# Layer 1's u, k, v and first two q tiles as seven-product quads behind four plain gate tiles, and fewer projection tiles left as filler for the attention and s5 stages

## The chip, the cores and the metric

One core of a Trainium2 chip runs the whole kernel. The metric is device time in microseconds of one launch. The core has a matrix engine (TensorE, PE in the profile; its weight loads are shown apart as PEld), three engines for element work (VectorE or DVE, ScalarE or ACT, GpSimd or POOL), a queue engine SyncE (SP), and DMA. Every engine works through its own instructions in order and waits for the others by semaphores.

## The reference

Two layers over 1024 tokens of width 1024, then a last RMSNorm. All is float32.

```python
hn = rmsnorm(h, norm1_g[layer]); proj = hn @ w_in[layer]      # 1024 x 3328
u, q, k, v = ...                                              # 512, 512, 128, 128 columns of proj
gate_a, gate_b = sigmoid(...), sigmoid(...)                   # 1024 columns each
y_a = s5_branch(u, ...)      # 32 groups of 16 channels, 64 complex states, a scan over the tokens in both
                             # directions, gelu to z, then z * sigmoid(z @ w_glu)
y_b = windowed_gqa(q, k, v, sink, bias, mask)                 # 8 query heads, 2 key heads, window 128
merged = gate_a * (y_a @ w_branch_a) + gate_b * (y_b @ w_branch_b)
h = h + merged @ w_out
hn2 = rmsnorm(h, norm2_g[layer])
h = h + (silu(hn2 @ ffn_w_gate) * (hn2 @ ffn_w_up)) @ ffn_w_down
```

## The kernel before

**Tiles and matmuls.** Activations lie with channels on the 128 partitions and tokens along the free side, in tiles of 128 channels by 512 tokens; the two halves of the tokens are h = 0 and 1. A float32 product is made of three matmuls on operands split into a high and a low part: high by high, low by high, high by low (L176 to L178 in `chain`, L187 to L189 in `piece`). One output tile of a projection, 128 columns of `w_in` by 512 tokens, is 8 k-tiles by 3 = 24 matmuls of 128x512. It is called an item here, `pj` in the profile; two items (both halves) share one weight block, a `Granule`.

**Weights.** A granule is 128x1024 of float32 (512 KB). SP loads it (L125, tile `raw`), ACT makes the high part (L164, `whi`), DVE the low part (L165, `wlo`). `emit` walks the list of items in order and keeps the split a few granules ahead (`ahead`) and the load further ahead (`fetch_to`). Plain float32 tiles live in 86 shared slots of 128x512.

**Quads.** In the FFN, a pair of weight blocks and both token halves are multiplied as a 2x2 block product with seven block products in place of eight. Each block product is 4 k-tiles by 3 = 12 matmuls, so a quad is 84 matmuls where four items are 96. It needs sums of weight blocks (`quad_part`, L139 to L153: tiles `sm`, `s3`, `s4`, `whs`, `wls`) and sums of activations (tiles `y`, then split into `tt`). Before the change only the FFN does this.

**Layer 1's first half, in the order of its list of items.** First the norm (`rs` on DVE at L89, psn on PE at L328 and L305), with the last products of layer 0's FFN (`dn`) laid between its steps. Then the projections k, v, q0, q1 and u0 as plain items. Then `attention_items`: 19 steps, each with score, softmax, transpose (`pt`) and value (`pv`) work, and `per * (i + 1)` filler items handed out in all by step i. Then `s5_items`.

**The s5 stage.** There are 16 states q and 8 outputs i, each output from two states. A state is eight small matmuls on PE (L943, `s5x`; 16 records in the trace), then on DVE nine instructions (L951 to L967) ending in `s5s`, then four copies on ACT (L971, `s5sg`). An output is twelve matmuls on PE (L985 to L988, `s5y`; 24 records); ACT squares and copies it (L990, L991), and its gelu goes DVE L1001 (`s5w`), ACT L1002, DVE L1009 (`s5g`). The result is stored to HBM (L1014, `zd`, four DMAs), and for the last two outputs SP issues those stores. One iteration of the loop holds two states and one output; the output belongs to states made two iterations earlier. Filler items stand between them, 2 for each iteration in layer 1.

**Behind the s5 stage.** `glu_items` loads z back (L1099, SP, `z<-zd`, eight DMAs, two for each of z0 to z3), ACT and DVE split it (`zp0h` to `zp3h` at L113, `zp0l` to `zp3l` at L114), and PE forms 8 glu tiles (96 matmuls), then the branch products `br`, whose operand `ybh` ACT casts (L860), then w_out.

**What sets the order.** The list of items is written by hand, and a scheduler lowers it to one instruction stream for each engine. Which item is filler where is set by the numbers `per` and by the order of the lists in `build`.

Of the kernel before, what the change touches and what calls it, by code (L numbers as in the profile page):

```python
# [8 lines left out]
F32 = mybir.dt.float32  # L9
# [4 lines left out]
ADD, SUB, MUL = ALU.add, ALU.subtract, ALU.mult  # L14
# [7 lines left out]
HC = 512  # L22
# [9 lines left out]
M_U, M_Q, M_K, M_V, M_GA, M_GB = 0, 4, 8, 9, 10, 18  # L32
# [16 lines left out]
R_BUFS = 4  # L49
# [47 lines left out]
class Trunk:  # L97
# [142 lines left out]
    def ahead(self, n):  # L240
        n = min(n, len(self.order))
        while self.split_ < n:

            g = self.order[self.split_]
            self.fetch_to(min(self.split_ + (R_BUFS if isinstance(g, QuadPart) else R_BUFS - 1), len(self.order)))
            self.parts(self.order[self.split_])
            self.split_ += 1

# [433 lines left out]
    apart = None  # L682

    def proj(self, l, m, done, xs=None):

        g = self.w_in(l, m)
        apart = self.apart
        st = {}

        def half(h):  # L690
            def run(part=None):
                if part != 1:
                    st[h] = self.PS(f"pj{m}")
                self.chain(st[h], g, 0, (xs or self.hn)[h], part)
# [173 lines left out]
    def attention_items(self, l, keys, q23, fill, per, tail):  # L868


        stage = {}
        fill = (list(fill[:2]) if l else []) + q23 + list(fill[2 if l else 0:])

        def scores(u):
            stage[u] = self.att_scores(l, u // 8, u % 8)
# [12 lines left out]
        for i in range(19):  # L888
# [232 lines left out]
        return early, split, out  # L1121


    def w_out_items(self, l):
        nc, V = self.nc, self.nc.vector
        self.h2 = {}
# [46 lines left out]
    def ffn_items(self, l, fill, head):  # L1173
# [6 lines left out]
        early = quads < 4  # L1180
# [56 lines left out]
        T = [[None] * 4 for _ in range(4)]  # L1237

        def sums(j):

            at = ((j, 0), (j, 1), (j + 4, 0), (j + 4, 1))
            if early:
                y11, y12, y21, y22 = (ys.pop(a) for a in at)
            else:
                y11, y12, y21, y22 = (self.A("y") for _ in at)
                for y, (m, h) in zip((y11, y12, y21, y22), at):
                    hi, lo = self.hn2[h][m]
                    V.tensor_tensor(y, hi.bitcast(F32), lo.bitcast(F32), ADD)
            V.tensor_tensor(y11, y12, y11, SUB)
            V.tensor_tensor(y12, y22, y12, SUB)  # L1250
            V.tensor_tensor(y22, y22, y11, SUB)
            V.tensor_tensor(y21, y21, y22, SUB)
            for k, y in enumerate((y11, y22, y12, y21)):
                T[k][j] = (y, None)

        def sum_pairs(j, k):
            T[k][j] = self.split(T[k][j][0], f"tt{k}")

        def quad_items(f):

            q = Quad(self.t["w_gate"][l, f].rearrange("p k c -> p (k c)"), self.t["w_up"][l, f].rearrange("p k c -> p (k c)"))
            b = {}

            def product(bank, g, off, xs, start):
                def run():
                    if start:
                        b[bank] = self.PS(f"q{bank}")
                    self.piece(b[bank], g, off, xs(), start)
                return (run, g)

            B = lambda h, a: lambda: self.hn2[h][a:a + 4]
            p = [product("x", q.a, 0, B(0, 0), True), product("y", q.b, HC, lambda: T[1], True),
                 product("v", q.b, 0, lambda: T[0], True), product("x", q.a, HC, B(0, 4), False),
                 product("y", q.c, 0, lambda: T[2], False), product("w", q.d, 0, lambda: T[3], True),
                 product("v", q.e, 0, B(1, 4), False)]

            def first():
                b["p1"] = self.A("qp")
# [101 lines left out]
    def build(self):  # L1380
# [31 lines left out]
        for l in range(DEPTH):  # L1412
# [23 lines left out]
            n0, n1 = (self.norm_parts(h, "ra", 2 * l, lambda m, h=h, src=src: src(m, h), lambda: self.hn) for h in range(2))  # L1436
            v1, v2 = self.halves(vc[0])
            loads, states = self.s5_head(l)
            tail_items = {12: pairs[:1] if l == 0 else []}
# [201 lines left out]
```

## Time and profile before

| | us |
|---|---|
| median of 3 runs | 2642.86 |
| lowest and highest run | 2641.52, 2645.24 |
| profiled execution, own time | 2646.65 |
| profiled execution, span of its trace | 2644.8 |
| PE busy | 2593.0 (98%) |
| DVE busy | 1660.2 (63%) |
| ACT busy | 1065.1 (40%) |

The span is the time from the first to the last instruction of the trace; the execution's own time is 1.85 us longer. Matmuls overlap, and their ends are modelled, so the busy time of PE is not the sum of their durations.

### The profile page before, as it was taken

How to read it: one execution, taken by the hardware profiler on the slowest of the kernel's cores; microseconds unless marked ns; L12 is line 12 of the kernel's file. 1: busy time of each engine (PE TensorE's matmuls, PEld its weight loads, DVE VectorE, ACT ScalarE, POOL GpSimd, SP SyncE). 2: the span in 40 equal slices, each digit the busy share in tenths (PEclk: the TensorE clock that was granted, in tenths of full speed). 3: DMA queues.
4: the chain of work that ended last, by engine and by line, in shares of the span. 5: the costliest groups of instructions: out<-in, count | busy, mean ns of one | idle time of the engine just before them, and what ended most of it. 6: DMA issues, size and time to landing. Idle time of an engine off the chain costs nothing.

```text
span 2644.8 us, 35127 instructions
## 1 busy us (share of the span) xinstructions
PE 2593.0 (98%) x12878; PEld 2109.6 (80%) x12878; DVE 1660.2 (63%) x3333; ACT 1065.1 (40%) x2053; POOL 359.8 (14%) x524
## 2 busy tenths in 40 slices
PE   8999999999999999999999999999999999999997
PEld 6787677887788888888877778888878888888886
DVE  8986877575986745544673465756376644654556
ACT  5336744422443433333344543453235433333332
POOL 0141001000142220121010001200002221122010
PEclk9999999999999999999999999999999999999998
DMA  3453435354274652564342245434315652455243
GB/s 139 131 186 123 136 117 183 118 189 143 60 191 118 124 107 60 115 127 91 103 151 76 72 140 171 149 128 159 128 64 114 133 124 64 90 121 114 59 110 134
DMA packets 157439, 321.36 MB, mean 122 GB/s; under 512 B 20769, under 2 KB 55841, under 8 KB 157265
## 3 DMA queue, kind: packets, MB, share of 16 engines
q1 hardware_dynamic: 106192, 201.68, 23.2%
q0 software_dynamic: 51072, 117.43, 20.4%
q8 instruction: 101, 1.65, 0.3%
q14 instruction: 74, 0.60, 0.1%
HBM read 196.37 MB, written 122.63 MB: 121 GB/s over the span
## 4 chain that ended last, share of the span: by engine, by line
PE 91%; DVE 5%; ACT 2%; DMA 1%; issue 1%; SPq 0%; DVEq 0%; ACTq 0%
PE pj L176 7%; PE pj L177 6%; PE pj L178 6%; PE dn L176 6%; PE dn L177 6%; PE dn L178 6%; PE qy L189 2%; PE qx L189 2%; PE qv L189 2%; PE qy L187 2%; PE qv L187 2%; PE qx L188 2%; PE qy L188 2%; PE qv L188 2%; PE qx L187 2%; PE br L176 2%
## 5 line engine op out<-in xcount | busy, mean ns | idle before, releaser
L165 DVE TENSOR_TENSOR wlo<-raw,whi 128x1024 fp32r<-128x1024 f32 (+3 forms) x210 | 186.5, 888 | 265.1 <-ACT whi L164 254.4
L164 ACT CAST whi<-raw 128x1024 fp32r<-128x1024 f32 (+3 forms) x210 | 163.6, 780 | 364.5 <-PE pj L177 116.5
L176 PE MATMUL pj<-rah,whi 128*128 128x512 f32 x768 | 307.4, 401 | 1.4 <-ACT rah L113 1.0
L177 PE MATMUL pj<-ral,whi 128*128 128x512 f32 x768 | 301.1, 392 | 1.3 <-DVE ral L114 1.3
L178 PE MATMUL pj<-rah,wlo 128*128 128x512 f32 x768 | 300.9, 392 | 0.0
L1220 POOL DMA_DIRECT2D hs<-dx x208 | 179.4, 872 | 854.6 <-ACT dx L1219 755.4
L176 PEld LDWEIGHTS pj<-rah,whi 128*128 128x128 f32 x768 | 145.2, 189 | 37.1 <-issue 4.8
L177 PEld LDWEIGHTS pj<-ral,whi 128*128 128x128 f32 x768 | 145.3, 189 | 31.5 <-DVE ral L114 3.2
L178 PEld LDWEIGHTS pj<-rah,wlo 128*128 128x128 f32 x768 | 145.0, 189 | 31.1
L1219 ACT COPY dx<-dn 128x512 f32<-128x512 f32 x208 | 120.9, 583 | 76.1 <-PE dn L178 75.4
L187 PE MATMUL qx<-rfh,whi 128*128 128x512 f32 x280 | 108.9, 389 | 0.0
L188 PE MATMUL qx<-rfl,whi 128*128 128x512 f32 x280 | 108.9, 389 | 0.0
L189 PE MATMUL qx<-rfh,wlo 128*128 128x512 f32 x280 | 108.9, 389 | 0.0
L799 DVE CUSTOM_DVE_ANT_0 x<-s,bias,nsink 128x384 f32<-128x384 f32 (+1 forms) x128 | 67.5, 580 | 64.0 <-PE s L793 63.7
L971 ACT COPY s5sg<-s5s 64x256 f32<-64x256 f32 x128 | 51.7, 404 | 128.9 <-DVE s5s L966 127.5
L176 PE MATMUL wo<-mgh,whi 128*128 128x512 f32 x256 | 100.0, 391 | 0.0
L178 PE MATMUL wo<-mgh,wlo 128*128 128x512 f32 x256 | 99.6, 389 | 0.0
L177 PE MATMUL wo<-mgl,whi 128*128 128x512 f32 x256 | 99.6, 389 | 0.0
L113 ACT CAST ffah<-ts 128x512 fp32r<-128x512 f32 x35 | 21.7, 621 | 190.3 <-DVE ts L1298 190.3
L176 PE MATMUL dn<-ffbh,whi 128*128 128x512 f32 x232 | 91.3, 394 | 0.0
L177 PE MATMUL dn<-ffbl,whi 128*128 128x512 f32 x232 | 90.6, 391 | 0.0
L177 PE MATMUL dn<-ffal,whi 128*128 128x512 f32 x232 | 90.4, 390 | 0.0
(431 smaller groups left out, 6711.2 us busy)
## 6 DMA issues: line engine op xcount, KB each, us to landing
hs<-dx POOLq DMA_DIRECT2D x208, 256.0 KB, 6.1
raw<-in_w_in SPq DMA_DIRECT2D x52, 512.0 KB
raw<-in_w_gate SPq DMA_DIRECT2D x44, 512.0 KB
raw<-in_w_up SPq DMA_DIRECT2D x44, 512.0 KB
raw<-in_w_down SPq DMA_DIRECT2D x96, 192.0 KB
g<-th POOLq DMA_DIRECT2D x64, 256.0 KB, 2.8
thr<-g SPq DMA_DIRECT2D x64, 256.0 KB
hs<-h POOLq DMA_DIRECT2D x48, 256.0 KB, 2.3
```

The lines of the kernel that those rows point to most:

```text
L164: nc.scalar.copy(g.hi[:, :n], g.raw[:, :n])
L165: nc.vector.tensor_tensor(g.lo[:, :n], g.raw[:, :n], g.hi[:, :n].bitcast(F32), SUB)
L176: mm(ps, lhsT=wh, rhs=xh, start=k == 0, stop=False)
L177: mm(ps, lhsT=wh, rhs=xl, start=False, stop=False)
L178: mm(ps, lhsT=wl, rhs=xh, start=False, stop=k == n - 1)
L187: mm(ps, lhsT=wh, rhs=xh, start=start and k == 0, stop=False)
L188: mm(ps, lhsT=wh, rhs=xl, start=False, stop=False)
L189: mm(ps, lhsT=wl, rhs=xh, start=False, stop=k == len(xs) - 1)
L799: V.tensor_tensor_reduce(out=x[:, :n], in0=ps[:, :n], in1=self.bias[hd][:, bo:bo + n], op0=ADD, op1=ALU.min, scale=-1.0, scalar=self.nsink ...
L971: nc.scalar.copy(SG[64 * r:64 * r + 64, g * 256:(g + 1) * 256].rearrange("p (d n) -> p d n", d=2), Sv[64 * g:64 * g + 64, :, r])
L1219: nc.scalar.copy(t, ps)
L1220: nc.gpsimd.dma_start(self.hs[m, h], t, accum_op=ADD)
```

## The change

**1. `ahead`.** For a plain granule the load is ordered up to two blocks ahead of the split and no longer three. Quad parts keep four.

**2. Layer 1's front.** `linear_quads` turns pairs of output tiles into quads: u0 with u1, u2 with u3, k with v, q0 with q1. It calls the existing tile functions with `grab` set, so that only their `done` functions (what is done with a finished tile) are taken. `sums` and `sum_pairs`, moved out of the FFN, make the activation sums for them, once for all four quads: 16 sums of `y` on DVE and 16 splits `tt`. In front of the quads stand four gate tiles gb0 to gb3, and no longer k and v, while the norm is made.

**3. Filler.** Before, the filler handed to the attention and s5 stages was q2, q3 (4 items), u1 to u3 (6 items) and all sixteen gate tiles (32 items): 42 items, 1 for each attention step and then 2 for each s5 iteration, 2 kept for glu. Now u is done earlier and so are four gate tiles: 28 items remain, 0.9 for each attention step (20 of them), then 1 for each s5 iteration (8), none for glu.

```diff
-            self.fetch_to(min(self.split_ + (R_BUFS if isinstance(g, QuadPart) else R_BUFS - 1), len(self.order)))
+            self.fetch_to(min(self.split_ + (R_BUFS if isinstance(g, QuadPart) else R_BUFS - 2), len(self.order)))
...
+        if self.grab is not None:
+            self.grab.append((m, done))
+            return []
...
-        fill = (list(fill[:2]) if l else []) + q23 + list(fill[2 if l else 0:])
+        fill = q23 + list(fill)
...
-            if i in (5, 7):
+            if i in (5, 7) and keys[-1]:
...
+    def linear_quads(self, l, made, T):
+
+        nc, V = self.nc, self.nc.vector
+        self.grab = tiles = []
+        for f in made:
+            f()
+        self.grab = None
+        out, nxt = [], []
+        for (m1, done1), (m2, done2) in zip(tiles[::2], tiles[1::2]):
+            p, b = self.quad_products(self.t["w_in"][l, m1], self.t["w_in"][l, m2], lambda: self.hn, T)
...
+        for k, (p, e) in enumerate(nxt):
+            if k == 0:
+                out.append(p[0])
+            out += [p[1], e[0], p[2], e[1], p[3], p[4], e[2], p[5], e[3]]
+            if k + 1 < len(nxt):
+                out.append(nxt[k + 1][0][0])
+            out += [e[4], p[6], e[5]]
+        return out
...
-                k1, k2 = self.halves(kc[0])
+                s = [(lambda j=j, T=T, ys=ys: self.sums(T, ys, self.hn, j),) for j in range(4)]
+                sp = [[(lambda j=j, k=k, T=T: self.sum_pairs(T, j, k),) for j in range(4)] for k in range(4)]
...
+                us = self.linear_quads(l, [lambda i=i: self.tile_u(l, i) for i in range(4)], T)
+                kvq = self.linear_quads(l, [lambda: self.tile_kv(l, M_K, kn), lambda: self.tile_kv(l, M_V, vn),
+                                            lambda: self.tile_q(l, 0), lambda: self.tile_q(l, 1)], T)
+                a, c = (self.halves(x) for x in (gb[0], gb[2]))
...
-                         [k1, n1[0], k2, v1, n1[1], n1[2], v2, n1[3], n1[4], n1[5], qc[0], ke[0], ve[0], qe[0], kc[1], ke[1],
-                          vc[1], ve[1]] + keys[:2] + [qc[1], qe[1], vals, bias0] + q1 + us[:2])
-                left = self.attention_items(l, keys, q23, us[2:] + gb + ga, 1, tail_items)
+                         [a[0], n1[0], a[1], c[0], n1[1], n1[2], c[1], n1[3], n1[4], n1[5], gb[4], *s[:2], gb[1], *s[2:], gb[3], *sp[1], gb[5],
+                          *sp[0], gb[6], *sp[2], gb[7], *sp[3]] + us + kvq[:15] + keys + kvq[15:17] + [vals] + kvq[17:] + [bias0])
+                left = self.attention_items(l, [None] * 4, q23, gb[8:] + ga, 0.9, tail_items)
...
-                left = self.s5_items(l, left, 2)
+                left = self.s5_items(l, left, 1)
```

(The lists `gb` and `ga` hold two items for each tile, one for each half; `gb[:8]` are the four tiles.) On PE the s5 stage of layer 1 now runs, from state 6 on: s5x(6), item, s5x(7), s5y(2), s5x(8), s5x(9), item, s5y(3), s5x(10), item, s5x(11), s5y(4), s5x(12), s5x(13), item, s5y(5), s5x(14), item, s5x(15), s5y(6), item, s5y(7), item, and then glu. On DVE, between the first instruction of state 6 and the last of state 15, stand ten states, four gelus and three low parts of weights. Before, PE had an item behind each s5x there, two behind s5y(6), and six between s5y(7) and glu.

The rows that follow are the instruction streams as they are ordered before and after the change; the changed file's line numbers are 3 higher there (L770 is L773, L990 is L993, L1002 is L1005) and 89 higher in the FFN. The first line of the change moves no row on any engine when it is made alone.

ScalarE in layer 1's s5 stage, around the sixth output, before: `s5sg<-s5s` are the copies of a state, `th<-pj` the end of a filler item, `s5g<-s5w` a gelu, `whi<-raw` the high part of a filler's weights.

```order
L1002 ACTIVATE s5g_15417<-s5w_15527 128x512
L770 ACTIVATE th1_15565<-pj12_15540 128x512
L990 ACTIVATE s5g_15588<-s5y_15574 128x512
L991 COPY s5yc_15587<-s5y_15574 128x512
L971 COPY s5sg_15617<-s5s_15611 64x256 x4
L770 ACTIVATE th0_15647<-pj13_15622 128x512
L971 COPY s5sg_15683<-s5s_15677 64x256 x4
L1002 ACTIVATE s5g_15588<-s5w_15688 128x512
L770 ACTIVATE th1_15716<-pj13_15691 128x512
L164 CAST whi_15773<-raw_15490 128x1024
```

The same stretch in the changed kernel:

```order
L993 ACTIVATE s5g_15815<-s5y_15801 128x512
L994 COPY s5yc_15814<-s5y_15801 128x512
L974 COPY s5sg_15844<-s5s_15838 64x256 x4
L974 COPY s5sg_15885<-s5s_15879 64x256 x4
L1005 ACTIVATE s5g_15815<-s5w_15890 128x512
L773 ACTIVATE th0_15928<-pj16_15903 128x512
L993 ACTIVATE s5g_15957<-s5y_15943 128x512
L994 COPY s5yc_15956<-s5y_15943 128x512
L164 CAST whi_16110<-raw_15932 128x1024
L974 COPY s5sg_15986<-s5s_15980 64x256 x4
```

Before, an end of a filler stands between any two groups of state copies; now one filler stands for two states, and two groups of copies follow one another.

ScalarE from the last output of layer 1's s5 stage on, before (`s5g<-s5y` is the last output's square, `zp0h<-z0` the first split of z):

```order
L990 ACTIVATE s5g_15828<-s5y_15814 128x512
L991 COPY s5yc_15827<-s5y_15814 128x512
L770 ACTIVATE th0_15856<-pj15_15831 128x512
L1002 ACTIVATE s5g_15828<-s5w_15866 128x512
L164 CAST whi_15934<-raw_15771 128x1024
L770 ACTIVATE th1_15894<-pj15_15869 128x512
L770 ACTIVATE th0_15928<-pj16_15903 128x512
L164 CAST whi_16034<-raw_15860 128x1024
L770 ACTIVATE th1_15963<-pj16_15938 128x512
L113 CAST zp0h_15979<-z0_15967 128x512
```

The same stretch in the changed kernel:

```order
L773 ACTIVATE th0_16104<-pj17_16079 128x512
L1005 ACTIVATE s5g_16073<-s5w_16076 128x512
L993 ACTIVATE s5g_16133<-s5y_16119 128x512
L994 COPY s5yc_16132<-s5y_16119 128x512
L164 CAST whi_16267<-raw_16108 128x1024
L773 ACTIVATE th1_16161<-pj17_16136 128x512
L1005 ACTIVATE s5g_16133<-s5w_16165 128x512
L113 CAST zp0h_16185<-z0_16173 128x512
L113 CAST zp0h_16189<-z0_16175 128x512
```

Before, one filler's end stands ahead of the last gelu, three stand behind it up to zp0h, and two more behind zp2h; now one stands ahead of it and none behind. ScalarE's line after zp2h then goes straight to the eight casts `ybh` and to zp3h; on VectorE the eight low parts `ybl` stand ahead of `zp3l` in both kernels.

SyncE's DMA issues from the store of the last but one output of layer 1's s5 stage on, before (`zd13` is the last quarter of z in HBM, `raw<-in_...` loads of weights):

```order
L1014 DMA zd13_12482<-s5g_15739 8x16x128 x4
L125 DMA raw_16032<-in_w_br_a 128x1024
L1014 DMA zd13_12482<-s5g_15828 8x16x128 x4
L125 DMA raw_16123<-in_w_br_b 128x1024
L1099 DMA z0_15967<-zd10_12479 128x512
L1099 DMA z0_15969<-zd10_12479 128x512
L1099 DMA z1_15971<-zd11_12480 128x512
L1099 DMA z1_15973<-zd11_12480 128x512
L1099 DMA z2_15975<-zd12_12481 128x512
L1099 DMA z2_15977<-zd12_12481 128x512
L125 DMA raw_16273<-in_w_br_a 128x1024
L1099 DMA z3_16038<-zd13_12482 128x512
L1099 DMA z3_16040<-zd13_12482 128x512
```

The same stretch in the changed kernel:

```order
L1017 DMA zd13_12480<-s5g_16073 8x16x128 x4
L1102 DMA z0_16173<-zd10_12477 128x512
L1102 DMA z0_16175<-zd10_12477 128x512
L1102 DMA z1_16177<-zd11_12478 128x512
L1102 DMA z1_16179<-zd11_12478 128x512
L1017 DMA zd13_12480<-s5g_16133 8x16x128 x4
L1102 DMA z2_16181<-zd12_12479 128x512
L1102 DMA z2_16183<-zd12_12479 128x512
L125 DMA raw_16611<-in_w_br_b 128x1024
L1102 DMA z3_16209<-zd13_12480 128x512
L1102 DMA z3_16211<-zd13_12480 128x512
```

Before, the loads of z0 to z2 follow the last store's four DMAs; now the loads of z0 and z1 stand ahead of those, and those of z2 and z3 behind.

At one more place VectorE's order differs: between the rows of the reciprocal root of layer 1's first half of the tokens (`rs`, L89) and the normed tiles `y` (L342) two sums of weight blocks of the first quad (`sm`, L139 and L140, 128x512) now stand, the first ahead of the last three `rs` rows, the second behind them.

## Rows read from the trace of the kernel before

**Rows 1.** Page of before: span; busy us of each engine (share, instructions); one group of section 5.
```profile
span 2644.8 us, 35127 instructions
...
PE 2593.0 (98%) x12878; PEld 2109.6 (80%) x12878; DVE 1660.2 (63%) x3333; ACT 1065.1 (40%) x2053; POOL 359.8 (14%) x524
...
L971 ACT COPY s5sg<-s5s 64x256 f32<-64x256 f32 x128 | 51.7, 404 | 128.9 <-DVE s5s L966 127.5
```

**Rows 2.** Timeline of PE in layer 1's front: start us, us, engine, line, what.
```profile
1375.62 0.39 PE L176 MATMUL pj<-rah,whi 128*128 128x512 f32 x1
...
1376.98 0.39 PE L176 MATMUL pj<-rah,whi 128*128 128x512 f32 x1
```

**Rows 3.** Windows: us, then busy us of PE, PEld, DVE, ACT, POOL; PEclk; DMA.
```profile
1380.00:1400.00 20.00, 20.00 (x94) 16.65 (x93) 3.68 (x3) 11.74 (x20) 0.00 (x0) 1.00 0.39 119
1639.55:1655.63 16.08, 16.08 (x105) 13.39 (x104) 13.23 (x29) 6.86 (x15) 3.62 (x6) 1.00 0.65 213
454.54:468.08 13.54, 10.79 (x62) 9.35 (x63) 11.88 (x27) 5.88 (x14) 2.37 (x4) 0.75 0.22 65
```

**Rows 4.** Timeline of DVE in layer 1's norm.
```profile
1341.16 0.68 DVE L296 TENSOR_TENSOR sqc<-sqc,sq 128x512 f32<-128x512 f32 x1
```

**Rows 5.** Timeline of PE in layer 1's norm; in brackets the idle time and its releaser.
```profile
1342.64 1.16 PE L328 MATMUL psn<-cst,rs 128*128 128x128 f32 x8 [0.94 <-DVE rs L89]
...
1359.49 0.63 PE L178 MATMUL pj<-rah,wlo 128*128 128x512 f32 x1
...
1365.46 0.63 PE L176 MATMUL pj<-rah,whi 128*128 128x512 f32 x1
```

**Rows 6.** Timeline of PE at a step of layer 0's attention.
```profile
299.77 0.65 PE L839 MATMUL pv<-p,vt 128*64 128x256 f32 x4 [1.54 <-ACT p L826]
```

**Rows 7.** Timeline of PE in one s5 iteration of layer 1.
```profile
1639.55 0.38 PE L985 MATMUL s5y<-s5uk 128*128 128x128 f32 x2
...
1642.32 1.10 PE L943 MATMUL s5x<-s5uk,s5wbt 128*64 128x128 f32 x16
1643.35 0.50 PE L176 MATMUL pj<-rah,whi 128*128 128x512 f32 x1
...
1649.01 1.10 PE L943 MATMUL s5x<-s5uk,s5wbt 128*64 128x128 f32 x16
```

**Rows 8.** Timeline of DVE in one s5 iteration of layer 0.
```profile
454.54 0.69 DVE L1001 SCALAR_TENSOR_TENSOR s5w<-s5g,s5yc 128x512 f32<-128x512 f32 x1
...
457.29 0.68 DVE L951 TENSOR_TENSOR s5a<-s5x,s5tb 128x512 f32<-128x512 f32 x1
...
462.68 0.68 DVE L951 TENSOR_TENSOR s5a<-s5x,s5tb 128x512 f32<-128x512 f32 x1
...
468.08 0.68 DVE L1001 SCALAR_TENSOR_TENSOR s5w<-s5g,s5yc 128x512 f32<-128x512 f32 x1
```

**Rows 9.** Timeline of DVE behind layer 1's s5 stage.
```profile
1732.07 1.23 DVE L165 TENSOR_TENSOR wlo<-raw,whi 128x1024 fp32r<-128x1024 f32 x1 [4.46 <-ACT whi L164]
```

**Rows 10.** Timeline of ACT behind layer 1's s5 stage.
```profile
1725.78 0.60 ACT L770 ACTIVATE th<-pj 128x512 f32<-128x512 f32 x1 [4.38 <-PE pj L178]
1726.27 0.62 ACT L1002 ACTIVATE s5g<-s5w 128x512 f32<-128x512 f32 x1
...
1748.03 4.78 ACT L860 CAST ybh<-yb 128x256 fp32r<-128x256 f32 x8
...
1753.47 0.61 ACT L113 CAST zp3h<-z 128x512 fp32r<-128x512 f32 x1
```

**Rows 11.** Timeline of SP's DMA issues behind layer 1's s5 stage.
```profile
1727.64 2.46 SPq L1014 DMA_DIRECT2D zd<-s5g  x4
...
1733.70 3.14 SPq L1099 DMA_DIRECT2D z<-zd  x6
```

**Rows 12.** The tile zd: time from issue to landing, layers 0 and 1.
```profile
DMA to landing us min/median/max: 2.0/2.8/5.8
```

More of the change, by code (lines that the diff above doesn't have):

```diff
@@ L680, in w_in @@
         return Granule(self.t["w_in"][l, m].rearrange("p k c -> p (k c)"), DM)
-    apart = None
+    apart = grab = None
     def proj(self, l, m, done, xs=None):
+        if self.grab is not None:
+            self.grab.append((m, done))
+            return []
         g = self.w_in(l, m)
@@ L1121, in glu_items, with sums @@
         return early, split, out
+    def sums(self, T, ys, pairs, j):
+        V = self.nc.vector
+        at = ((j, 0), (j, 1), (j + 4, 0), (j + 4, 1))
+        if ys is not None:
+            y11, y12, y21, y22 = (ys.pop(a) for a in at)
+        else:
+            y11, y12, y21, y22 = (self.A("y") for _ in at)
+            for y, (m, h) in zip((y11, y12, y21, y22), at):
+                hi, lo = pairs[h][m]
+                V.tensor_tensor(y, hi.bitcast(F32), lo.bitcast(F32), ADD)
+        V.tensor_tensor(y11, y12, y11, SUB)
+        V.tensor_tensor(y12, y22, y12, SUB)
+        V.tensor_tensor(y22, y22, y11, SUB)
+        V.tensor_tensor(y21, y21, y22, SUB)
+        for k, y in enumerate((y11, y22, y12, y21)):
+            T[k][j] = (y, None)
@@ new lines, in sum_pairs, with quad_products, product, run @@
+    def sum_pairs(self, T, j, k):
+        T[k][j] = self.split(T[k][j][0], f"tt{k}")
+    def quad_products(self, src1, src2, pairs, T):
+        q = Quad(*(s.rearrange("p k c -> p (k c)") for s in (src1, src2)))
+        b = {}
+        def product(bank, g, off, xs, start):
+            def run():
+                if start:
+                    b[bank] = self.PS(f"q{bank}")
+                self.piece(b[bank], g, off, xs(), start)
+            return (run, g)
+        B = lambda h, a: lambda: pairs()[h][a:a + 4]
+        return [product("x", q.a, 0, B(0, 0), True), product("y", q.b, HC, lambda: T[1], True),
+                product("v", q.b, 0, lambda: T[0], True), product("x", q.a, HC, B(0, 4), False),
+                product("y", q.c, 0, lambda: T[2], False), product("w", q.d, 0, lambda: T[3], True),
+                product("v", q.e, 0, B(1, 4), False)], b
@@ new lines, in linear_quads, with first, second, out11 @@
+    def linear_quads(self, l, made, T):
[7 more added lines that the diff above has]
+            p, b = self.quad_products(self.t["w_in"][l, m1], self.t["w_in"][l, m2], lambda: self.hn, T)
+            def first(b=b):
+                b["p1"] = self.A("qp")
+                nc.scalar.copy(b["p1"], b["x"])
+            def second(b=b):
+                b["u2"] = self.A("qu")
+                V.tensor_tensor(b["u2"], b["p1"], b["y"], ADD)
+            def out11(b=b, done=done1):
+                done(0, b["x"])
+            def sum22(b=b):
+                V.tensor_tensor(b["p1"], b["p1"], b["y"], ADD)
+                b["c22"] = self.A("qc")
+                V.tensor_tensor(b["c22"], b["p1"], b["v"], ADD)
+            def out2(b=b, done=done2):
+                V.tensor_tensor(b["p1"], b["p1"], b["w"], ADD)
+                done(0, b["p1"])
+                done(1, b["c22"])
+            def out12(b=b, done=done1):
+                V.tensor_tensor(b["u2"], b["u2"], b["v"], ADD)
+                done(1, b["u2"])
+            nxt.append((p, [(fn,) for fn in (first, second, out11, sum22, out2, out12)]))
+        for k, (p, e) in enumerate(nxt):
[6 more added lines that the diff above has]
+        return out
@@ L1239, in sums @@
         def sums(j):
[L1241 to L1254, printed above, removed]
+            self.sums(T, ys, self.hn2, j)
         def sum_pairs(j, k):
-            T[k][j] = self.split(T[k][j][0], f"tt{k}")
+            self.sum_pairs(T, j, k)
         def quad_items(f):
[L1261 to L1275, printed above, removed]
+            p, b = self.quad_products(self.t["w_gate"][l, f], self.t["w_up"][l, f], lambda: self.hn2, T)
             def first():
@@ L1435, in build @@
             src = (lambda m, h: xs[h][m]) if l == 0 else (lambda m, h: self.h2[m, h])
-            n0, n1 = (self.norm_parts(h, "ra", 2 * l, lambda m, h=h, src=src: src(m, h), lambda: self.hn) for h in range(2))
+            ys, T = {}, [[None] * 4 for _ in range(4)]
+            n0, n1 = (self.norm_parts(h, "ra", 2 * l, lambda m, h=h, src=src: src(m, h), lambda: self.hn, ys if l else None)
+                      for h in range(2))
             v1, v2 = self.halves(vc[0])
```

3 lines of the change are left out of this document (added).

## The prediction

> **What bounds the kernel now.** First the page: PE is busy 2593.0 of 2644.8 us [rows 1], so a change pays if it takes matmuls away, and costs if it opens a gap on PE. Next PE's timeline in layer 1's front, for the price of one matmul: seven in a row start from 1375.62 to 1376.98 [rows 2], so 0.227 us from one start to the next, though each shows 0.39; they overlap, and the spacing is what a removed one gives back. Then the windows, stage by stage, since the change takes work from one stage and puts it into another. In an s5 iteration of layer 1 PE is busy the whole 16.08 us and DVE 13.23 [rows 3]: PE is the bound there, but by only 2.85 us. In layer 0's s5 stage, where the filler is smaller, an iteration took 13.54 us with PE at 10.79 and DVE at 11.88 [rows 3]; the reader is to see that there PE waits. Last, the timelines of DVE, ACT and SP behind the s5 stage, because that chain is covered by filler which the change takes away.
>
> **What the quads give.** Four quads of 84 matmuls replace 4 x 96. 48 x 0.227 = **10.9 us less** on PE. TensorE's share is certain, since the list of instructions is shorter. The Trainium skill, "TensorE: Matmul & The Clock Gate", section "Back-to-back issue gap", gives about 131 ns for a matmul of 512 columns in a sustained stream of weight loads and matmuls; by that figure the gain would be an estimated 6.3 us and the sum below 4.6 us higher. This trace does not agree: its spacing is 227 ns in a full stream.
>
> **What the quads add in the front.** VectorE gets 76 more instructions there (16 sums, 16 low parts `tt`, 36 for four quads' weights less 8 of the plain blocks, 20 for the quads' ends, and 4 fewer elsewhere): by the 0.68 us of a 128x512 sum [rows 4] some 52 us. They lie beside eight plain items (8 x 5.66 = 45 us, below) and four quads (336 x 0.227 = 76 us), 121 us in which VectorE had little to do: 3.68 of 20 us [rows 3]. Priced at nothing; if that cover failed for one quad, PE would wait for some ten of those rows, 7 us. Two of the added sums are not covered: L139 and L140 of the first quad stand in and behind the reciprocal root for which PE already waits 0.94 us [rows 5], and ahead of the normed tiles. 2 x 0.6 = **+1.2 us** (0 to 1.4).
>
> **Attention.** 20 items on 19 steps at 0.9 leaves two steps (4 and 15) without one. Steps of layer 0 without filler left PE waits of up to 1.54 us [rows 6]. Two such: **+2 us** (0 to 4).
>
> **The s5 stage.** PE's price for each part is in one iteration of layer 1 [rows 7]: s5y 2.77 (1639.55 to 1642.32), s5x 1.03 (to 1643.35), item 5.66 (to 1649.01). With one item an iteration is 2.77 + 2 x 1.03 + 5.66 = 10.5 us of PE. VectorE's price is in layer 0, where it runs without a break [rows 8]: gelu with its wait for ScalarE 2.75 (454.54 to 457.29), one state 5.39 (to 462.68), so 2 x 5.39 + 2.75 = 13.5, plus a low part of weights, 1.23 [rows 9], every other iteration. **VectorE becomes the bound.** The loss is not 3 us times the iterations, for outputs lag states by two iterations and PE may fall behind in its favour only until that lead is used up. So I sum the run from state 6 to the start of the last output. PE: ten s5x, six items, five s5y = 10.3 + 34.0 + 13.9 = 58.2. VectorE: 1.03 until state 6 is there, ten states, four gelus, three low parts = 1.03 + 53.9 + 11.0 + 3.7 = 69.6, then four state copies of 0.404 [rows 1] on ScalarE, 71.2. The difference is **+13 us** on PE. Lower bound: VectorE's rows at their busy time alone, 13.23 for two states, a gelu and a low part [rows 3]; five times that, less two low parts, is 63.7, with the ends 66.3, so +8. Upper bound: the three low parts also wait for ScalarE, whose queue holds the two groups of state copies in front of their high parts (3 x 1.2 more): +17. I take the middle, since layer 0's rows are this very loop.
>
> **From the last output to glu.** The filler that covered this chain has gone. Count from the end E of the last item, which stands behind s5y(7). ScalarE must do that item's `th` before the last gelu; in the trace the gelu starts 0.49 us behind the start of `th`, and the store of it on SP starts 1.86 behind [rows 10, 11]. Four stores take 2.46 to issue: E + 4.3. Landing takes 2.0 to 2.8 us from the issue [rows 12], so zd is there at about E + 6. z2's two loads are issued behind those stores (0.52 each, 3.14 / 6 [rows 11]) and land, priced like zd's, at E + 7; two splits of 0.61 [rows 10], then eight `ybh` casts, 4.78 us [rows 10], now stand ahead of `zp3h`: E + 13. High and low part of zp3 make it E + 14. PE can do the nine matmuls on z0 to z2 before, 2 us: PE is idle **+12 us** (9, if the casts find room while z lands; 14 with the slower landing and no matmul ahead). Before, six items (34 us) lay over all this. The Trainium skill, "DMA: Bandwidth & Descriptors", section "Anatomy of one DMA", gives about 2.0 us as the fixed part of one DMA; the trace's minimum agrees, its median of 2.8 does not, and by the page's figure the chain would be an estimated 1.6 us shorter.
>
> **The clock.** Behind the gap in layer 1's norm, matmuls take 0.63 and not 0.39 from 1359.49 to 1365.46, ten of them [rows 5], and the window of layer 0's s5 stage shows PEclk 0.75 [rows 3]: it falls to the lower level after PE has stood. A cluster costs ten times 0.2 to 0.24. One behind the gap before glu and a part of one in the s5 stage, where VectorE sets the time anyway: **+3 us** (2 to 7).
>
> **The other edits.** The fetch line moves no row when it stands alone. The key and value tiles made earlier lie beside the quads. Both nothing.
>
> **Sum.** -10.9 + 1.2 + 2 + 13 + 12 + 3 = +20.3. On the profiled execution's 2646.65 that is 2667; that execution lies 3.8 above the median of the runs, so for the median 2642.86 + 20.3 = **2663 us**. Bounds together: -10.9 + 0 + 0 + 8 + 9 + 2 = +8 (2651), and -10.9 + 1.4 + 4 + 17 + 14 + 7 = +32 (2675).
>
> **Rivals.**
> 1. The other side, faster: PE stays the bound in the s5 stage. It would be so if VectorE's iteration stayed under PE's 10.5 us or if the states made early outlast the stage, so that s5y never waits, and if the z chain overlapped the last item (z0 to z2 come early, only z3 late, 3 us). For it: VectorE had 2.85 us to spare in each 16.08 [rows 3]. Against: 13.23 busy does not go into 10.5. Time: -10.9 + 1.2 + 3 = -7, 2636. It decides at a VectorE lag under about 4 us in all.
> 2. Half of it: the lead takes up the lag in the s5 stage, but the chain before glu stays open. -10.9 + 1.2 + 2 + 12 + 2 = +6, 2649. For it: six states are made in the attention steps; against: two iterations' lead is 6 us at 3 each, and the stage has nine.
> 3. Worse: the front's quads wait for their weights' sums as well, 7 us for each of two, +34, 2677. For it: 76 more VectorE rows; against: VectorE's idle windows [rows 3].
> 4. The quads don't give what they say, as matmuls that wait for sums are no shorter stream, while filler still covers the rest: no change, 2643. The trace speaks against it, for the spacing is that of full streams.
>
> **Chances.** The forecast 0.72, rival 1 0.09, rival 2 0.10, rival 3 0.06, rival 4 0.03. Range: the forecast's bounds, widened to rival 2 below and 3 us upwards towards rival 3: 2649 to 2678. About 0.2% (5.3 us) is what a measurement here can tell from no change. Faster: rival 1, 0.09. Same: rival 4 and the third of rival 2 that would end below 2648, 0.06. Slower: the rest, 0.85.
>
> **What would show it.** Right: in the s5 stage of layer 1 DVE without idle time and PE waiting at L943 or at s5y's rows for `s5sg`, with iterations of 13 to 14.5 us; one PE gap of some 10 us before the first glu rows that need zp3, released by zp3h or zp3l; slow matmuls behind it; u's quads without waits. Wrong: PE full in the s5 stage, s5y(7) no later than 58 us behind state 6, or waits in the front larger than these.

## The result: 25 us slower, 0.94%

The changed kernel takes 2668.99 us (median; 2668.63 to 2669.70), before 2643.4 (2641.52 to 2645.24): a ratio of 1.0094, interval 1.0082 to 1.0106; the two medians lie 25.6 us apart. The profiled execution of the changed kernel, 2668.63, lies at its median; that of before, 2646.65, lay 3.8 above its own. Of that, more below, for it hides what the change costs in the norm.

The page has 48 matmul records fewer and 80 VectorE records more (I had counted 76), and PE's busy time hardly moved while the span grew by 22.0 us [rows 1]:

```profile
span 2666.8 us, 35161 instructions
...
PE 2590.6 (97%) x12830; PEld 2105.4 (79%) x12830; DVE 1708.8 (64%) x3413; ACT 1083.4 (41%) x2085; POOL 359.5 (13%) x524
```

PE's waits by releaser (us in total, times, longest). Those of before were 5.5 for `s5uk<-ud`, all in layer 0, 7.0 for `rs`, and none for glu:

```profile
PE s5x L946 <- DMA s5uk<-ud: 15.7, 3, 5.7
PE psn L328 <- DVE rs L89: 10.6, 4, 4.3
...
PE s5x L946 <- DVE sm L802: 4.9, 3, 3.8
PE glu L176 <- ACT zp0h L113: 3.3, 1, 3.3
...
PE glu L176 <- ACT zp2h L113: 2.8, 1, 2.8
```

**The quads** are worth what was said. The first 24 of their 28 products run without a gap from 1404.09 to 1469.37, 65.28 us, so 2.72 each for 12 matmuls or 0.2267 us a matmul, the spacing of [rows 2].
The Trainium skill, "TensorE: Matmul & The Clock Gate", section "Back-to-back issue gap", gives about 131 ns for a matmul of 512 columns in a sustained stream; the changed kernel's trace again says 227 for its float32 parts.

**The s5 stage.** Windows from one state's first VectorE row to that of a later one (us; busy us of PE, PEld, DVE, ACT, POOL; PEclk; DMA share; GB/s), and last the stretch from the end of the last filler item to the first branch product. Before, an iteration was 16.08 us long and PE was full [rows 3]:

```profile
1684.35:1700.14 15.79, 10.86 (x84) 9.12 (x86) 13.12 (x28) 6.07 (x14) 2.61 (x5) 0.95 0.61 200
1700.14:1713.68 13.54, 13.54 (x84) 11.35 (x81) 11.88 (x27) 4.82 (x12) 2.44 (x4) 0.81 0.70 218
1713.68:1728.72 15.04, 9.95 (x80) 8.34 (x80) 13.11 (x28) 6.85 (x15) 3.58 (x6) 0.91 0.57 183
1728.72:1742.28 13.56, 13.56 (x86) 11.48 (x86) 11.89 (x28) 4.83 (x12) 2.39 (x4) 0.85 0.47 149
1763.90:1796.55 32.65, 26.31 (x99) 19.46 (x98) 23.29 (x36) 22.20 (x37) 0.58 (x1) 0.84 0.29 98
```

The reader is to see VectorE's busy time, 13.1 of 15 us or 11.9 of 13.5, nearly the same sum as in layer 0's loop: its rows go on with hardly a pause but the wait for ScalarE inside each gelu (1.46 us). PE is busy only 10 to 11 of 15 to 16 us in the windows that hold its two waits. The last output starts 72.7 us behind state 6 (1683.20 to 1755.86), where I had summed 71.2. On PE's timeline both waits are attributed to the loads of a state:

```profile
1699.82 1.97 PE L946 MATMUL s5x<-s5uk,s5wbt 128*64 128x128 f32 x16 [4.93 <-DMA s5uk<-ud]
...
1728.57 1.98 PE L946 MATMUL s5x<-s5uk,s5wbt 128*64 128x128 f32 x16 [5.09 <-DMA s5uk<-ud]
```

**Behind the s5 stage** the same four rows as in [rows 10], at ScalarE: the last gelu directly behind the last item's `th`, the casts in front of zp3h:

```profile
1764.92 0.59 ACT L773 ACTIVATE th<-pj 128x512 f32<-128x512 f32 x1
1765.40 0.62 ACT L1005 ACTIVATE s5g<-s5w 128x512 f32<-128x512 f32 x1
...
1774.43 4.79 ACT L863 CAST ybh<-yb 128x256 fp32r<-128x256 f32 x8
1779.13 1.14 ACT L113 CAST zp3h<-z 128x512 fp32r<-128x512 f32 x2
```

and at SP the stores (`zd`) of the last two outputs, the loads of z0 and z1 between them, and those of z2 and z3 behind:

```profile
1759.42 3.69 SPq L1017 DMA_DIRECT2D zd<-s5g  x4
1763.22 1.84 SPq L1102 DMA_DIRECT2D z<-zd  x4
1766.90 2.44 SPq L1017 DMA_DIRECT2D zd<-s5g  x4
1769.58 0.80 SPq L1102 DMA_DIRECT2D z<-zd  x2
...
1771.38 0.79 SPq L1102 DMA_DIRECT2D z<-zd  x2
```

PE meets the chain twice: z0's load goes out only behind the four stores of the last output but one, and z2's only behind those of the last. PE runs at the lower level of its clock behind each gap (0.8 where 0.39 was usual):

```profile
1767.41 0.79 PE L176 MATMUL glu<-zp0h,whi 128*128 128x512 f32 x1 [3.26 <-ACT zp0h L113]
...
1773.58 0.80 PE L176 MATMUL glu<-zp2h,whi 128*128 128x512 f32 x1 [2.80 <-ACT zp2h L113]
...
1779.79 0.73 PE L176 MATMUL glu<-zp3h,whi 128*128 128x512 f32 x2 [0.28 <-ACT zp3h L113]
```

The stretch takes 32.65 us where 21.76 lay between glu's start and the branch products before (1752.78 to 1774.54): 10.9 more, 6.3 of them waiting and the rest in matmuls at the lower clock.

### The profile page after: what moved, and what is told of

Read it like the earlier page. It is cut to its first block, busy times and chain, and to the rows that moved or that the text cites. A ratio compares the mean times of both kernels' runs of the same rounds, so it can differ in the third digit from the quotient of the medians.

```text
span 2666.8 us, 35161 instructions
## 1 busy us (share of the span) xinstructions
PE 2590.6 (97%) x12830; PEld 2105.4 (79%) x12830; DVE 1708.8 (64%) x3413; ACT 1083.4 (41%) x2085; POOL 359.5 (13%) x524
## 4 chain that ended last, share of the span: by engine, by line
PE 89%; DVE 5%; DMA 2%; ACT 2%; issue 1%; SPq 0%; DVEq 0%; ACTq 0%
PE dn L176 6%; PE dn L177 6%; PE dn L178 6%; PE pj L176 5%; PE pj L177 5%; PE pj L178 5%; PE qx L187 3%; PE qx L189 3%; PE qx L188 3%; PE qy L187 3%; PE qv L189 3%; PE qy L189 3%; PE qy L188 3%; PE qv L188 3%; PE qv L187 3%; PE br L176 2%
## 5 line engine op out<-in xcount | busy, mean ns | idle before, releaser
L165 DVE TENSOR_TENSOR wlo<-raw,whi 128x1024 fp32r<-128x1024 f32 (+3 forms) x202 | 176.7, 875 | 224.0 <-ACT whi L164 218.5
L164 ACT CAST whi<-raw 128x1024 fp32r<-128x1024 f32 (+3 forms) x202 | 155.5, 770 | 334.8 <-PE pj L177 85.1
L176 PE MATMUL pj<-rah,whi 128*128 128x512 f32 x640 | 257.4, 403 | 0.7 <-ACT rah L113 0.7
L177 PE MATMUL pj<-ral,whi 128*128 128x512 f32 x640 | 251.8, 394 | 1.3 <-DVE ral L114 1.3
L178 PE MATMUL pj<-rah,wlo 128*128 128x512 f32 x640 | 251.3, 393 | 0.0
L176 PEld LDWEIGHTS pj<-rah,whi 128*128 128x128 f32 x640 | 121.7, 190 | 31.1 <-issue 5.3
L177 PEld LDWEIGHTS pj<-ral,whi 128*128 128x128 f32 x640 | 121.8, 190 | 26.8 <-DVE ral L114 3.0
L178 PEld LDWEIGHTS pj<-rah,wlo 128*128 128x128 f32 x640 | 121.4, 190 | 26.2
L775 POOL DMA_DIRECT2D g<-th x64 | 35.9, 561 | 411.9 <-ACT th L773 411.7
```

The source lines that it names most:

```text
L164: nc.scalar.copy(g.hi[:, :n], g.raw[:, :n])
L165: nc.vector.tensor_tensor(g.lo[:, :n], g.raw[:, :n], g.hi[:, :n].bitcast(F32), SUB)
L176: mm(ps, lhsT=wh, rhs=xh, start=k == 0, stop=False)
L177: mm(ps, lhsT=wh, rhs=xl, start=False, stop=False)
L178: mm(ps, lhsT=wl, rhs=xh, start=False, stop=k == n - 1)
```

## Experiments

Times are medians; the changed kernel is 2669.0, before 2642 to 2644 in each set.

**1. The filler's place alone, without quads.**

```diff
-  ... + [qc[1], qe[1], vals, bias0] + q1 + us[:2])
-  left = self.attention_items(l, keys, q23, us[2:] + gb + ga, 1, tail_items)
+  ... + [qc[1], qe[1], vals, bias0] + q1 + us + gb[:8])
+  left = self.attention_items(l, keys, q23, gb[8:] + ga, 0.9, tail_items)
...
-  left = self.s5_items(l, left, 2)
+  left = self.s5_items(l, left, 1)
```

> The kernel before, without any quad: u, k, v, q0, q1 stay plain items, but u1 to u3 and the four gate tiles gb0 to gb3 are run ahead of attention, so that attention and the s5 stage of layer 1 get the same 28 items at the same rates as in the changed kernel (0.9 a step, 1 an iteration, none left for glu). The theory that the loss is from where the filler stands (VectorE's run in the s5 stage, the open chain before glu, two bare attention steps) expects the changed kernel plus the 10.9 us that the quads save, less some 1 to 2 us of the norm and the quads' own waits: about 2678 us, 34 us above before. The rival, that the quads themselves cost (sums of weights in the norm, VectorE's added rows, their evictions), expects the time of before within 6 us: 2640 to 2650.

2675.6 us, ratio 1.0124 (1.0109 to 1.0139): 34 us slower without a single quad. PE's waits in it are those of the changed kernel:

```profile
PE s5x L943 <- DMA s5uk<-ud: 11.3, 2, 5.8
...
PE glu L176 <- ACT zp0h L113: 2.4, 1, 2.4
PE glu L176 <- ACT zp2h L113: 2.3, 1, 2.3
```

So the loss is the filler's place. The distance to the changed kernel is 6.6 us and not 10.9 less 1 or 2; the norm, below, is the main difference.

**2. More filler for the s5 stage and the end: the second branch's products.**

```diff
-  left = self.s5_items(l, left, 1)
+  self.add(pairs)
+  left = self.s5_items(l, left + bb, 2.6)
...
-  ... early[3:] + (pairs[:1] if l else []) + left[n // 2:n] + split[3:] + (self.mix(glu, pairs[1:]) if l else glu)
+  ... early[3:] + left[n // 2:n] + split[3:] + glu
...
-  rest = left + [it for p in zip(bb, ba) for it in p]
+  rest = left + ba
```

> The changed kernel with the sixteen products of the second branch (2.9 us each, 47 us in all, which stand behind glu in the changed kernel) given to the s5 stage as filler too, at 2.6 items an iteration, and what is left of them before glu. Nothing else is taken away. If the loss is filler missing beside VectorE's run and before glu, the waits of PE there (5, 5 and 6.3 us, and the slow matmuls behind them) are filled with work that has to be done anyway: minus 18 to 26 us, 2643 to 2651. If the stage is held by SP's queue or by the quads, the s5 stage still stands at its loads and the gain is under 8 us: 2661 or more.

2652.0 us (1.0034, 1.0020 to 1.0048): 17 us of the 25.6 come back, one less than the low end that I gave. The waits in layer 1's s5 stage shrink to one of 2.5 us; glu waits once, 1.43 us; the 3.84 us wait at the end of attention and the norm's 4.3 stay. The edit does one thing more than the expectation says: `self.add(pairs)` moves the splits `ybh` and `ybl` from the chain in front of zp3h to the head of the s5 stage. What the filler and what this move gave at the end, the run doesn't tell apart; run 7 covers the end by filler alone.

**3. Loads of a state ahead of the weight block.**

```diff
+  if more and l:
+      self.item(lambda q=2 * j + 3: load(q))
   filler(i + 0.5)
...
-  if more:
+  if more and not l:
       self.item(lambda q=2 * j + 3: load(q))
   filler(i + 1)
```

> The changed kernel with one edit: in layer 1 the loads of an iteration's second state are issued beside those of its first, so that the loads of states 9 and 13 no longer stand behind a weight block's load on SP. In the changed kernel PE waits 4.9 and 5.1 us just there, by the trace for those loads. If VectorE's run sets the pace (its rows stand without a break from 1691 to 1757), the two waits go and others of the same sum appear in front of an output or a state: 0, between minus 2 and plus 2. If SP's queue sets it: minus 8 to minus 12 us, 2657 to 2661.

2680.9 us: 12 slower, which neither reading expected. The weight block's load now stands in front of the loads of both states of the next iteration. DVE, SP and PE in that run:

```profile
1725.05 1.23 DVE L165 TENSOR_TENSOR wlo<-raw,whi 128x1024 fp32r<-128x1024 f32 x1 [3.14 <-ACT whi L164]
```

```profile
1726.30 0.34 SPq L125 DMA_DIRECT2D raw<-in_w_br_b  x1
...
1728.59 1.17 SPq L931 DMA_DIRECT2D s5uk<-ed  x2
```

```profile
1733.26 1.98 PE L946 MATMUL s5x<-s5uk,s5wbt 128*64 128x128 f32 x16 [5.20 <-DMA s5uk<-ud]
1737.14 1.12 PE L946 MATMUL s5x<-s5uk,s5wbt 128*64 128x128 f32 x8 [1.91 <-DMA s5uk<-ud]
```

VectorE makes the low part at 1725.05, having waited 3.14 us for the high part; SP's load of the next block, which waits for that buffer, goes out at 1726.30; the states' loads follow it, and PE's two waits for them end at 1733.26 and 1737.14. Four such waits in this stage sum to 14.5 us, and from its first output to its last it takes 94.4 us against 86.2: 8.2 of the 12. It is a loop: PE's item holds a weight buffer, ScalarE's high part waits for it, VectorE's low part for that, SP for the low part, the states' loads for SP, and PE for the loads. In this run VectorE stands in its middle, and the end of the stage was reordered too (a z load stood ahead of the first store): the waits in glu sum to 8.7 us, in the changed kernel to 6.3. So the run shows that SP's line matters, but doesn't tell the two bounds apart; runs 4 to 6 do.

**4. The branch weights' loads on another queue.**

```diff
-  self.nc.sync.dma_start(g.raw[:, :g.n], g.src)
+  (self.nc.gpsimd if g.pool else self.nc.sync).dma_start(g.raw[:, :g.n], g.src)
...
+  g.pool = l == 1 and name != "w_glu"
```

> The changed kernel with the loads of layer 1's eight branch weight blocks issued by GpSimd's queue and no longer by SP's, so that no load of a state's tables can stand behind a weight block that waits for a buffer. The order on PE, VectorE and ScalarE is the changed kernel's. If VectorE's run alone sets the pace of the s5 stage, the waits at states 9 and 13 move to other rows: minus 2 to plus 2 us. If SP's queue is the bound by itself, the 10 us of those waits and the slow matmuls behind them go: minus 9 to minus 13. The run with the loads moved by half an iteration got slower by 12 us, so a third reading is that both are coupled (a late load holds PE, PE holds a weight buffer, the weight's high part holds VectorE): then minus 3 to minus 8.

2671.2 us: 2 us slower, most of it outside the trace, whose span is 2667.5 against 2666.8. In layer 1 PE no longer waits for loads; it waits for `s5sg`, the end of a state, in front of the outputs, 11.2 us in place of 10.0:

```profile
1726.43 0.49 PE L991 MATMUL s5y<-s5sg,s5ca 128*128 128x127 f32 x2 [2.56 <-ACT s5sg L975]
...
1739.96 0.49 PE L991 MATMUL s5y<-s5sg,s5ca 128*128 128x127 f32 x2 [2.67 <-ACT s5sg L975]
...
1748.11 0.49 PE L991 MATMUL s5y<-s5sg,s5ca 128*128 128x127 f32 x2 [1.07 <-ACT s5sg L975]
...
1754.64 0.80 PE L991 MATMUL s5y<-s5sg,s5ca 128*128 128x127 f32 x2 [4.92 <-ACT s5sg L975]
```

Two iterations take VectorE 28.2 us, in the changed kernel 28.6 (1700.14 to 1728.72):

```profile
1699.88:1728.10 28.22, 25.60 (x196) 21.89 (x196) 24.88 (x54) 11.67 (x26) 6.59 (x11) 1.00 0.67 209
```

(PE runs ahead in this window: it holds 196 matmul records, and two iterations of the stage have 160.) The waits moved and the pace stayed: with SP's line out of the way, VectorE alone gives it.

**5. Lighter states.**

```diff
-  V.tensor_tensor(bv, zv[:, :, ::-1], s, MUL)
-  V.tensor_tensor(Sv[:, :, 0], Sv[:, :, 0], bv[:, :, 0], SUB)
-  V.tensor_tensor(Sv[:, :, 1], Sv[:, :, 1], bv[:, :, 1], ADD)
+  if l == 0:
+      (the same three lines)
```

> The changed kernel with layer 1's states made lighter on VectorE: three of the nine instructions of a state (the product with the second table row and the two sums, L968 to L970, 1.4 to 1.5 us for a state) are left out, so the states are not the reference's. Two states and a gelu then take 10.6 us on VectorE against 10.5 us on PE. If VectorE sets the pace, ten states between state 6 and the last output lose 14 us, of which PE can take what it waits, 10 us of waits and 3 of slow matmuls: minus 9 to minus 13. If VectorE is not the bound there: minus 3 to 0.

2663.3 us, 5.7 less, of the 9 to 13 expected. Two iterations still take 28.5 us, though VectorE is busy only 19.6 of them; it waits 2.80 us for each high part, and PE for the loads as before:

```profile
1695.85:1724.32 28.47, 23.87 (x160) 19.95 (x160) 19.62 (x42) 11.77 (x26) 6.02 (x10) 0.86 0.64 200
```

```profile
1716.07 1.23 DVE L165 TENSOR_TENSOR wlo<-raw,whi 128x1024 fp32r<-128x1024 f32 x1 [2.80 <-ACT whi L164]
```

The gain isn't in the s5 stage. The profiled execution is 3.8 us shorter, 3.3 of them in attention, where the wait at its end falls from 3.84 to 1.93 us; from the first output to the last the stage takes 86.4 us, in the changed kernel 86.2. So there is a second bound at the same height, the loop of run 3.

**6. Both at once.** The edits of runs 4 and 5.

> Both of the two before it at once: branch weights loaded by GpSimd's queue, and three of a state's nine VectorE instructions left out in layer 1 (the states are not the reference's). Alone, the one moved the waits to the outputs and the other left them at the loads of states 9 and 13, each with the pace of the changed kernel (28.6 and 28.5 us for two iterations). If there are two bounds of nearly the same height, VectorE's run and the loop of SP's loads, a weight buffer and its low part on VectorE, then only both together free PE: the waits in the s5 stage fall from 10 to under 3 us, minus 11 to minus 16 against the changed kernel, 2653 to 2658. If something else holds the stage (ScalarE's copies, the loads' landing), no more than the lighter states gave alone: 2661 to 2664.

2658.1 us, 10.9 less than the changed kernel, 5.2 less than run 5. Two of VectorE's iterations now take 26.3. PE's own two take 20.8 there (state 8 to state 12, 1687.96 to 1708.80), so PE runs ahead, full, through this window (203 matmul records, where two iterations have 160), and pays at the last output, with one wait of 6.24:

```profile
1693.63:1719.90 26.27, 26.27 (x203) 22.78 (x203) 19.54 (x42) 11.67 (x26) 6.59 (x11) 1.00 0.71 220
```

```profile
1744.03 0.80 PE L992 MATMUL s5y<-s5sg,s5ca 128*128 128x127 f32 x2 [6.24 <-ACT s5sg L976]
```

The two bounds are there: with one of them taken away the pace stays at 28, with both it falls to 26.3. But they are not all of it. The waits in the stage did not fall under 3 us as I expected: VectorE's iterations are still longer than PE's, since each low part waits 2.80 us for a high part, which stands behind a state's copies on ScalarE:

```profile
1708.88 1.66 ACT L976 COPY s5sg<-s5s 64x256 f32<-64x256 f32 x4 [3.31 <-DVE s5s L968]
1710.56 1.05 ACT L165 CAST whi<-raw 128x1024 fp32r<-128x1024 f32 x1
```

That is the wait of my upper bound in the prediction's sum. And of the 10 us by which the profiled execution is shorter, the s5 stage has 6.5 (79.7 us from its first output to its last, in place of 86.2) and attention 4.9, while the chain in front of the branch products got 3.0 longer.

**7. Two items for the end.** `0.9` becomes `0.8` in the call of `attention_items`.

> The changed kernel with 0.8 in place of 0.9 items for each attention step: two items go from attention to the end, so that three items and no longer one stand between the last output's gelu and glu. The stretch from the last item to the branch products takes 32.7 us against 21.8 before. If the open chain costs those 11 us, the waits for zp0h and zp2h (3.3 and 2.8) and the slow matmuls behind them go: minus 9 there, plus 2 for two more attention steps without an item, so minus 7 (minus 4 to minus 10), 2659 to 2665. If the chain's waits would only move (loads of z held by stores and weights), no change.

2655.0 us: 14 less, twice what I expected. Glu starts without a wait and the branch products 22.9 us behind it; and the wait at the end of attention is gone as well, though three steps (the third, eighth and thirteenth) are now without an item where two (the fifth and sixteenth) were:

```profile
1618.65 1.10 PE L946 MATMUL s5x<-s5uk,s5wbt 128*64 128x128 f32 x16 [0.95 <-ACT th L773]
```

```profile
1760.94 1.07 PE L176 MATMUL glu<-zp0h,whi 128*128 128x512 f32 x4
...
1770.94 0.73 PE L176 MATMUL glu<-zp3h,whi 128*128 128x512 f32 x2 [0.65 <-ACT zp3h L113]
```

**8. Which step is bare.** `round(per * (i + 1))` becomes `round(per * (i + 1) + 0.3)`.

> The changed kernel with the same 20 items on the 19 attention steps, but rounded so that the one step without an item is the ninth, and no longer the fifth and the sixteenth. If the 3.8 us wait of PE at 1626.94 and the slow matmuls behind it come from the bare sixteenth step, where the states' work already lies beside attention's: minus 4 to minus 6 us. If a bare step costs up to 1.5 us wherever it stands, as I priced it: minus 1 to minus 2. If the wait belongs to the end of attention whatever the filler: 0.

2664.1 us: 4.9 less. The wait at that place is 0.94:

```profile
1628.68 1.10 PE L946 MATMUL s5x<-s5uk,s5wbt 128*64 128x128 f32 x16 [0.94 <-ACT th L773]
```

It was 3.84 with PE's slow clock behind it (16 records in 1.97 us, before 1.10):

```profile
1626.94 1.97 PE L946 MATMUL s5x<-s5uk,s5wbt 128*64 128x128 f32 x16 [3.84 <-DVE sm L802]
```

A bare step costs next to nothing early in attention and 5 us at its sixteenth, where the first states already lie on VectorE; run 7, with bare steps only up to the thirteenth, agrees.

**9. Both refills.** The edits of runs 2 and 7.

> The changed kernel with both refills: 0.8 items for each attention step, and the second branch's products as filler of the s5 stage at 2.6 items an iteration and in front of glu. All work of the reference is there. If the parts add up, the gain of the quads stays (10.9 us) less what is left of waits in the norm (3.4 more than before), in the front (1.1) and in attention (about 1): 5 us below before, 2635 to 2642. If filler beside VectorE's run brings VectorE more work (the branch's splits and low parts) and PE waits for that in place: 2645 to 2655.

2638.9 us: a ratio of 0.9983 to before (0.9974 to 0.9993). It beats both kernels, inside the range I gave if the parts add up. The kernel before with the same refill and without quads was not run, so the 4 us are those of quads and refill together. Windows of run 9's layer 1 s5 stage up to glu, PE full in all:

```profile
1660.00:1700.00 40.00, 40.00 (x234) 33.56 (x233) 30.73 (x60) 22.86 (x43) 6.78 (x12) 1.00 0.59 199
1700.00:1740.00 40.00, 40.00 (x253) 33.11 (x253) 30.35 (x62) 16.32 (x33) 8.48 (x15) 1.00 0.61 194
1740.00:1789.23 49.23, 49.23 (x282) 41.62 (x279) 26.94 (x51) 23.42 (x45) 5.00 (x9) 1.00 0.38 119
```

**10. The norm.** Run 9 with `R_BUFS = 5`, `N_SLOTS = 84` and the loads' distances kept.

> The run with both refills (2638.9 us) and with five buffers for raw weight blocks in place of four, for two slots fewer (84), the loads ordered as far ahead as before. In the instruction streams the two sums of the first quad's weights then no longer stand between the rows of the reciprocal root in layer 1's norm. If those sums, and the load that the first of them waits for, cost the norm what its wait shows (4.3 us in the changed kernel against 0.9 before), minus 2 to minus 4 us: 2635 to 2637. If the norm's wait is made by the products around it, or the fewer slots cost elsewhere: 0 to plus 4.

2637.9 us, 0.9975 to before (0.9965 to 0.9985), 0.9 under run 9, which the spread of the two (2637.3 to 2640.6, 2633.0 to 2639.9) doesn't part. The wait for `rs` in layer 1's norm fell to 0.85 us, but one of 2.11 came ahead of it, for a sum of squares (`sqc`), with eleven slow matmuls behind. VectorE's row shows why: the first sum of weights still waits for its block, now in front of the last rows of that sum of squares.

```profile
1332.87 0.69 DVE L139 TENSOR_TENSOR sm<-raw 128x512 f32<-128x512 f32 x1 [3.15 <-DMA raw<-in_w_in]
```

So the wait that a sum brings moved with it, and PE's wait with that. What the norm would cost without the sums, the run doesn't show.

## Why the prediction was right, point by point

- **The quads, -10.9.** Right, by the spacing above.
- **The front at nothing.** Nearly: one wait of 1.1 us, for ScalarE's copy at the end of a quad.
- **The norm, +1.2. This step was mis-sized: it is +5.6.** I priced two sums at their duration. The first of them waits for its weight block, 2.82 us, with the reciprocal root's rows behind it on VectorE, and PE waits 4.33 in place of 0.94 [rows 5]:

```profile
1342.65 0.69 DVE L139 TENSOR_TENSOR sm<-raw 128x512 f32<-128x512 f32 x1 [2.82 <-DMA raw<-in_w_in]
1343.26 0.15 DVE L89 TENSOR_TENSOR rs<-rs 128x4 f32<-128x4 f32 x1
```

```profile
1344.82 2.07 PE L328 MATMUL psn<-cst,rs 128*128 128x128 f32 x8 [4.33 <-DVE rs L89]
```

The rest is matmuls at the lower clock behind that wait. Windows over the norm, from the end of the last product in front of its sum of squares to the first item behind it, in the changed kernel, in before's profiled execution and in run 1, whose norm has before's instructions:

```profile
1334.53:1368.61 34.08, 27.60 (x124) 22.40 (x123) 24.39 (x57) 10.65 (x18) 5.05 (x10) 0.90 0.39 152
1336.51:1367.34 30.83, 28.04 (x124) 22.61 (x122) 22.54 (x54) 9.56 (x16) 3.78 (x7) 0.89 0.41 162
1335.11:1363.59 28.48, 25.02 (x122) 20.17 (x123) 23.09 (x55) 10.06 (x17) 4.51 (x9) 1.00 0.45 176
```

Against run 1 the norm costs 5.6 us: 3.0 more of waits, 2.6 of slow matmuls. Against before's profiled execution it looks like 3.3, because that execution ran its own ten slow matmuls there [rows 5]: 2.4 of the 3.8 us by which it lies above its median. Every profile with the changed norm (the changed kernel and runs 2 to 9) shows 33.7 to 34.8. That most runs of before lack such a cluster is read from their times and mean granted clocks, not seen: of the 34 taken beside the experiments, 18 lie under 2643.6 us, 17 of them at 0.994 to 0.996, and 11 above 2645, 9 of them at 0.992 or 0.993; the profiled one is at 0.991. The term is 4.4 us larger than I gave it, and its bound was 1.4.
- **Attention, +2.** Size off, above its bound of 4: about +4.6 (waits of 4.7 us where before had 1.8, and slow matmuls). It isn't two bare steps at 1 us; one of them costs all of it (run 8).
- **The s5 stage, +13.** Right in size: state 6 to the last output takes 72.7 us against PE's own 58.2, so +14.5, waits of 10.0 us and about 4 of slow matmuls behind them. VectorE's pace was the one I summed. That PE's waits stand at the loads of states 9 and 13 was not foreseen: SP's loop is a second bound within 1% of VectorE's (28.5 and 28.2 us alone), so taking away either changes next to nothing in the stage (84.8 and 86.4 us from its first output to its last, against 86.2).
- **The chain before glu, +12 of idle time. Near in size by luck: 10.9, but 6.3 of waits and 4.6 of slow matmuls.** The chain itself is about as long as I counted (zp3h starts at 1779.13, 15 us behind the end of the last item; I had 13), and the casts stood ahead of zp3h as said. But I gave PE only nine matmuls to do meanwhile, and it went on with further glu tiles' products on z0 to z2: only 0.28 us of waiting for zp3h, no gap of some 10 us. It waited where I had put nothing, 3.26 for zp0h and 2.80 for zp2h, whose loads stand behind stores on SP. The Trainium skill, "DMA: Bandwidth & Descriptors", section "Anatomy of one DMA", puts the fixed part of a DMA on GpSimd's path at about 2.0 us; the issues in this chain are SP's, and over both engines' the landing times of zd were 2.1 at least, 2.6 in the median and 6.8 at most, so the figure is near the floor here.
- **The clock, +3. This term was mis-sized most: some 13 us**, twice its upper bound of 7. It is in the sums above: about 2 in attention, 4 in the s5 stage, 4.6 before the branch products, 2.6 in the norm. I gave a whole cluster to one gap and part of one to another; every gap of 2.8 us and more in layer 1 had one.

Sum with the measured terms: -10.9 + 5.6 + 1.1 + 4.6 + 14.5 + 10.9 = 25.8, against 25.6 between the medians. Put the other way: I forecast 28 us of waits and 3 of slow matmuls; the waits came to some 23 and the slow matmuls to 13. The mechanism, filler gone from beside VectorE's run and from the chain before glu, is shown by runs 1, 2 and 7; that the total came within 6 us is in part these two errors against each other.

Rivals 1 and 2 needed the lead of the states to last, which it didn't; rival 3's waits in the front did not come; rival 4 is gone with the quads' spacing and with run 1.

## What to carry to other kernels

Work that is off the path in one stage can be the cover of the next: before taking matmuls out of a list, ask which stage they were filling, and how long the other engines need there with the cover gone. Here 10.9 us of saved work cost 30 us of lost cover and nearly 7 of new waits, slow matmuls included; with other work (products that had to be done anyway) in the place of the filler the kernel was 4 to 6 us faster than before. A wait names who came last, not the bound: two bounds of one height show no gain in their stage when either is removed. A gap costs more than it lasts, so price the slow matmuls behind each one that you expect. And an instruction moved into a chain costs its own wait as well as its duration.

## What the runs showed of the hardware

Each gap of 2.8 to 5.1 us on PE in layer 1 of the changed kernel was followed by 3 to 9 matmuls of 512 columns at the lower level of its clock, 1.2 GHz (0.63 us where 0.39 was usual; PEclk fell to 0.81 in a window behind such a wait, and stayed at 1.00 in that of run 4, whose wait there was 2.56 us). Shorter waits went either way. A wait of 1.93 us at the end of attention in run 5 was followed by PEclk 0.75 (1623.30 to 1630.00), one of 1.94 at the same place in run 6 by 1.00 (1622.60 to 1630.00). And the same two short waits in layer 1's norm (1.04 and 0.8 us) were followed by ten slow matmuls in before's profiled execution and by none in run 1's, with the same instructions there: the norm took 30.8 us in the one and 28.5 in the other.
